# A two-layer hybrid block whose helper engines are held to a planner's order to the end of both layers

## The chip, the cores and the metric

The kernel runs on one core of a Trainium2 chip. The metric is device time in microseconds (us) from the start to the end of one execution; lower is better. The kernel before takes 1624.94 us, the median of three runs from 1623.77 to 1626.47. Five engines are named below: TensorE (PE, matmuls), VectorE (DVE), ScalarE (ACT), GpSimd (POOL) and SyncE (SP, which issues the transfers).

## What is computed

The reference runs two layers over 512 latent tokens and 256 context tokens of width 1024. Each layer mixes tokens (layer 0 with windowed attention, layer 1 with differential attention) and then runs a squared-ReLU MLP. Modulation vectors for shift, scale and gate come from a conditioning vector.

```python
def sqrelu_mlp(h, w1, w2):
    return jnp.square(jax.nn.relu(h @ w1)) @ w2

for i in range(DEPTH):
    mod_x = jax.nn.silu(c) @ w_ada[i] + b_ada[i]
    sh1, sc1, g1, sh2, sc2, g2 = jnp.split(mod_x[:, None, :], N_MOD, axis=-1)
    hx = x * (1.0 + sc1) + sh1
    ax, ac = window_gqa(...) if i % 2 == 0 else diff_attention(...)
    x = layer_norm(alpha * x + g1 * ax, ln1_g[i], ln1_b[i])
    fx = sqrelu_mlp(x * (1.0 + sc2) + sh2, mlp_w1[i], mlp_w2[i])
    x = layer_norm(alpha * x + g2 * fx, ln2_g[i], ln2_b[i])
    # layer 0: the same for the context tokens, with their own modulation
```

All data are float32. The MLP is 1024 to 4096 to 1024.

## The kernel before, in words

Every float32 product is made of three matmuls. A weight tile is brought in as `w_raw`, ACT casts it to the rounded format `w_h` (line 318), DVE subtracts to get the remainder `w_l` (line 324), and `mm3` (lines 335 to 337) multiplies w_h by the rounded activations, w_l by the same, and w_h by the remainder of the activations. So each weight needs one ACT and one DVE instruction before PE can use it.

Both MLPs work on 6 blocks of 128 tokens in layer 0 (4 of latents and 2 of context) and 4 in layer 1. Their first products partly use a scheme with fewer multiplications (Strassen-like): sums of weight tiles (`w_sum`, made by POOL at line 278) and sums of activations (`hx_sum`) are multiplied instead of the tiles, and the results (`h_ps`) are put together by adds (`relu<-h_ps`). The weights of that part are half tiles of 512 columns, `w_half`, cast at line 771 and split at line 773. The second product (`y_ps`) adds into `fx`, block by block. `y_weights(c, half)` asks for the weights of the second product of part c.

At the end of a layer's MLP, `last_y` does this: for the halves that are already complete, `fold` lets POOL compute fx times the gate row and add it to `acc` (alpha * x); `final` then takes the last piece of the second product from PSUM, multiplies it by the gate row (`g_tmp`, line 594) and adds it to acc; then come the statistics (`bn`, `mv`, `rstd`; the power of `rstd` is taken by POOL), the normalisation (line 545) and, in layer 0, the transposes `xn_t` (line 560) which feed the next layer's projections (`qkv_ps`). The gate row is made from the modulation `mods` by a transpose on PE (`gate_t`, line 467), a store to `gate_d` and a load as a row on all partitions (`g`). The modulation of the layer's second part and of layer 1 is itself computed on DVE beside the MLP of layer 0, by custom instructions on `w_raw` with the conditioning vector (`CUSTOM_DVE` at line 684, shown as ISA in orders of instructions).

The order of the work is made by a planner when the program is built. A class `Flow` runs through the jobs with estimated durations, for PE's time T and for queues A (ACT), D (DVE), G (POOL) and Q (SP). A `Ring` counts the free buffers of a tag in this plan. Where `fl.pin` names an engine and an instruction was given with `ins`, the plan's order becomes a hard order on that engine; with `fl.loose` the weight conversions are given without `ins`, so they are placed by program order and data alone. In the kernel before, `loose` is set in layer 0 after the first products of the MLP, and in layer 1 `pin` is emptied there.

Of the kernel before, what the change touches and what calls it, by code (L numbers as in the profile page):

```python
# [13 lines left out]
F32 = mybir.dt.float32  # L14
# [5 lines left out]
P = 128  # L20
# [47 lines left out]
class Flow:  # L68
# [177 lines left out]
def hybrid_block(ctx: ExitStack, tc: tile.TileContext, t: dict, out: bass.AP):  # L246
# [63 lines left out]
    def wsplit(src, n=1024, raw=None, hl=None, pool=False):  # L310
        if raw is None:
            raw = raw_tile()
        if hl is None:
            hl = [wpool.tile([P, 1024], F32R, name="w_" + x, tag="w" + x, bufs=NH) for x in "hl"] + [rwh.get(), rwh]
        raw, rg, rr = raw
        h, l, hg, hr = hl
        q = dma(n, [rg], out=raw[:, :n], in_=src)
        last["cast"] = nc.scalar.copy(out=h[:, :n], in_=raw[:, :n])  # L318
        a = fl.op("A", act(n), [q, hg], ins=None if fl.loose else last["cast"])
        kw = dict(out=l[:, :n], in0=raw[:, :n], in1=f(h)[:, :n], op=ALU.subtract)  # L320
        if pool:
            d = gp(pool2(n), [a], nc.gpsimd.tensor_tensor, **kw)
        else:
            last["split"] = nc.vector.tensor_tensor(**kw)  # L324
# [3 lines left out]
        rel.ring = hr  # L328
        return Weight(h, l, d, rel)

    last = {}

# [188 lines left out]
    def bcast_load(pool, src, nm, c0=0, n=BC):  # L521
        b = pool.tile([P, D], F32, name=nm, tag="bc", bufs=n)
        reload(b, src, c0)
        return b
# [195 lines left out]
    def mlp_pipe(l, hx, ready, ntok, acc, get_gates, done, fx, T, R):  # L720
# [40 lines left out]
        def part_sums(q):  # L761
            (a1, g1, f1), (a2, g2, f2) = R.pair_raws(q)
            q1 = dma(1024, [g1], out=a1, in_=t["w1"][l, 2 * q])
            q2 = dma(1024, [g2], out=a2, in_=t["w1"][l, 2 * q + 1])
            ws = R.sum_tile()
            (a11, a12), (a21, a22), (s1, s2) = [(x[:, 0:512], x[:, 512:1024]) for x in (a1, a2, ws)]

            def half(src, dep):
                nhalf[0] += 1
                w = R.half_tile(nhalf[0] - 1)  # L770
                a = nc.scalar.copy(out=w[:, 0:512], in_=src)  # L771
                a = fl.op("A", act(512), [dep, R.rhalf.get()], ins=None if fl.loose else a)
                d = nc.vector.tensor_tensor(out=w[:, 512:1024], in0=src, in1=f(w)[:, 0:512], op=ALU.subtract)  # L773
                d = fl.op("D", dve(512), [a], ins=None if fl.loose else d)
                rel = Task()
                rel.ring = R.rhalf
# [139 lines left out]

        gates, st, Wy, fresh, folds = [], {}, {}, set(), {}

# [57 lines left out]
        def last_y():  # L976
            def final(half, tb, pt, p, slot):
                r = gated_add(R.pool, lambda x: sm_.give(slot, x), acc[tb], half, pt, p, gates[0 if tb < NXB else 1],
                              half == 1 or l == 0, more=[folds[half, tb]])
                st[tb], r = stats(acc[tb], half, r, st.get(tb))  # L980
# [19 lines left out]
            yield from before(1)  # L1000
            halves = (1,) if gates else (0, 1)
            if not gates:
                gates.extend((yield from get_gates()))
            for half in halves:
                for tb in range(ntb):
# [62 lines left out]
        if l:  # L1068
            yield from plain(range(4), cuts)
            yield from plain((4, 5), [slice(0, ntok)], sums, 4)  # L1070
        else:
            yield from plain((0, 1), cuts, step=R.step)
            R.swap()
            for ft in range(2, 6):
                yield from plain((ft,), [t1, t2], sums, (3, 3, 2, 1)[ft - 2])
            for _ in sums:
                pass
        y_weights(0, 0)
        if l == 0:
            y_weights(0, 1)  # L1080
        if l == 0:
            fl.loose = True
        else:
            fl.pin = ""
        weights(3, 4)
        y_weights(0, 1)
        yield from steps(R.first)
        for q in range(3, 16):
            if q == R.gate_at:
                gates += yield from get_gates()  # L1090
            if q == 4 and l == 0:
                st2["second"] = True
# [421 lines left out]
    with tc.tile_pool(name="mlp0", bufs=1, reuse_waits="tile") as pool:  # L1514
# [33 lines left out]
        class R0:  # L1548
            rhalf = Ring(fl, 3)
            first, mixes = 2 * NTB, ((2, 2, 2, 0), (2, 5, 5, 0), (4, 4, 4, 0))  # L1550
# [9 lines left out]
            def half_tile(self, n):  # L1560
                p_, tag, b = ((pool, "bc", 2), (wpool, "wh", NH), (wpool, "wl", NH))[n % 3]
                return p_.tile([P, 1024], F32R, name="w_half", tag=tag, bufs=b)

# [98 lines left out]
    with tc.tile_pool(name="attn1", bufs=1, reuse_waits="tile") as pool:  # L1662
        EB1, XB1, SB = 5, 3, 1
        fl.loose = False
        fl.pin = "DAG"
# [342 lines left out]
    with tc.tile_pool(name="mlp1", bufs=1, reuse_waits="tile") as pool:  # L2008
# [37 lines left out]
        class R1:  # L2046
            rhalf, rbc = Ring(fl, 4), Ring(fl, 1)
            first, mixes = 4, ((2, 1, 2, 1), (2, 2, 2, 2), (2, 2, 2, 2))
# [17 lines left out]
            def half_tile(self, n):  # L2066
                p_, tag, b = (pool, "half", 3) if n % 4 else (late, "wl", 1)
                return p_.tile([P, 1024], F32R, name="w_half", tag=tag, bufs=b)

# [98 lines left out]
```

## Time and profile before

| what | value |
|---|---|
| median of three runs | 1624.94 us (1623.77 to 1626.47) |
| the profiled execution | 1628.53 us, span 1626.7 us |
| PE busy | 1570.4 us (97%) |
| DVE busy | 1144.1 us (70%), 2202 instructions |
| ACT busy | 790.2 us (49%) |
| POOL busy | 443.5 us (27%), 364 instructions |
| mean granted clock of PE | 0.992 |

In the trace, layer 0's MLP runs from about 385 to 885 us, with its reduced products until 825; layer 1's MLP runs from about 1263 to the end. The profile gives, per engine, busy time, idle time and the instruction that ended an idle time ("<-"). A window is a stretch of the span; its columns are the busy times of PE, of PE's weight loads, of DVE, ACT and POOL, then the granted clock (1.00 is full speed), the share of the DMA engines in use, and GB/s. In a timeline a row gives the start, the duration, the engine, the line and operation, output and inputs, and in brackets the idle time before it with what ended it.

### The profile page before, as it was taken

Reading aid. Unit: us, or ns where it says so; the run is one execution under the profiler, and the core shown is the slowest. Engines: PE = TensorE matmul, PEld = TensorE weight load, DVE = VectorE, ACT = ScalarE, POOL = GpSimd, SP = SyncE. Lnnn points to the kernel's source line nnn. Section 1 sums busy time; section 2 is a strip of 40 time slices with the busy share of each in tenths; the row PEclk is TensorE's granted clock in tenths of the full one; section 3 lists DMA queues with packets and bytes.
Section 4 is the critical chain, followed back from the end, with each engine's and each line's share of the span. In section 5 each row is a group of like instructions: output and inputs, shape, how many; then the busy total and the mean of one; then the engine's idle time right before and its main releaser. Section 6 shows DMA issues by size and latency. Waiting matters only on the chain.

```text
span 1626.7 us, 25214 instructions
## 1 busy us (share of the span) xinstructions
PE 1570.4 (97%) x9465; PEld 1376.0 (85%) x9465; DVE 1144.1 (70%) x2202; ACT 790.2 (49%) x1679; POOL 443.5 (27%) x364
## 2 busy tenths in 40 slices
PE   7999999999999999999998999999999999999998
PEld 5887777689888888888987999999987889889896
DVE  4665676689686678967567777777765796655667
ACT  3465675465334333433525655556552655554450
POOL 1344453203211221112162123220101163222363
PEclk9999999999999999999999999999999999999999
DMA  9111551352345434444243222211132333333321
GB/s 376 47 53 34 182 169 52 120 181 99 127 141 170 143 118 148 161 131 143 91 162 118 64 72 72 72 49 40 40 110 98 117 104 104 104 104 104 104 69 61
DMA packets 66435, 181.18 MB, mean 111 GB/s; under 512 B 7368, under 2 KB 13320, under 8 KB 66312
## 3 DMA queue, kind: packets, MB, share of 16 engines
q1 hardware_dynamic: 66312, 179.56, 32.9%
q8 instruction: 74, 1.21, 0.3%
q14 instruction: 49, 0.40, 0.1%
HBM read 168.49 MB, written 11.04 MB: 110 GB/s over the span
## 4 chain that ended last, share of the span: by engine, by line
PE 48%; DVE 6%; POOL 4%; ACT 2%; issue 2%; DMA 1%; SPq 0%; DVEq 0%; POOLq 0%; ACTq 0%
PE y_ps L335 6%; PE y_ps L336 6%; PE y_ps L337 6%; PE h_ps L335 5%; PE h_ps L336 5%; PE h_ps L337 5%; PE qkv_ps L335 3%; PE qkv_ps L336 3%; PE qkv_ps L337 3%; PE s_ps L1819 2%; PE o_ps L1857 2%; POOL acc L278 1%; PE pT_ps L1885 1%; POOL w_raw L278 1%; DVE acc L272 1%
## 5 line engine op out<-in xcount | busy, mean ns | idle before, releaser
L335 PE MATMUL y_ps<-w_h,hid 128*128 128x512 f32 (+1 forms) x648 | 257.5, 397 | 2.8 <-ACT w_h L318 1.8
L336 PE MATMUL y_ps<-w_l,hid 128*128 128x512 f32 (+1 forms) x648 | 256.8, 396 | 1.8 <-DVE w_l L324 1.8
L337 PE MATMUL y_ps<-w_h,hid 128*128 128x512 f32 (+1 forms) x648 | 256.4, 396 | 0.0
L324 DVE TENSOR_TENSOR w_l<-w_raw,w_h 128x1024 fp32r<-128x1024 f32 (+1 forms) x133 | 159.9, 1212 | 55.8 <-ACT w_h L318 53.8
L318 ACT CAST w_h<-w_raw 128x1024 fp32r<-128x1024 f32 (+1 forms) x133 | 130.9, 1000 | 111.2 <-PE y_ps L337 94.4
L337 PEld LDWEIGHTS y_ps<-w_h,hid 128*128 128x128 f32 x648 | 123.3, 190 | 29.1
L335 PEld LDWEIGHTS y_ps<-w_h,hid 128*128 128x128 f32 x648 | 123.5, 191 | 28.7 <-ACT w_h L318 2.6
L336 PEld LDWEIGHTS y_ps<-w_l,hid 128*128 128x128 f32 x648 | 123.3, 190 | 27.6 <-DVE w_l L324 2.9
L773 DVE TENSOR_TENSOR w_half<-w_raw,w_half 128x512 fp32r<-128x512 f32 x130 | 104.1, 808 | 59.3 <-ACT w_half L771 58.9
L771 ACT CAST w_half<-w_raw 128x512 fp32r<-128x512 f32 x130 | 79.6, 620 | 129.1 <-PE h_ps L337 91.7
L278 POOL TENSOR_TENSOR w_sum<-w_raw 128x512 f32<-128x512 f32 x26 | 45.2, 1739 | 315.6 <-DMA w_raw<-in_w 228.7
L335 PE MATMUL qkv_ps<-w_h,hx 128*128 128x384 f32 (+1 forms) x384 | 127.8, 333 | 0.3 <-ACT w_h L318 0.3
L278 POOL TENSOR_TENSOR e<-e,sm 128x512 f32<-128x512 f32 (+2 forms) x96 | 93.5, 990 | 113.8 <-DVE sm L272 81.6
L336 PE MATMUL qkv_ps<-w_l,hx 128*128 128x384 f32 (+1 forms) x384 | 122.6, 319 | 1.1 <-DVE w_l L324 1.1
L337 PE MATMUL qkv_ps<-w_h,hx 128*128 128x384 f32 (+1 forms) x384 | 122.1, 318 | 0.0
L278 POOL TENSOR_TENSOR w_raw<-w_raw,w_sum 128x512 f32<-128x512 f32 x26 | 52.4, 2016 | 187.2 <-DVE w_half L773 169.6
L684 DVE CUSTOM_DVE_ANT_0 w_raw<-w_raw,cB 128x512 f32<-128x512 f32 x112 | 90.0, 831 | 15.6 <-PE y_ps L337 13.9
L272 DVE TENSOR_TENSOR fx<-y_ps,fx 128x512 f32<-128x512 f32 x110 | 75.1, 685 | 27.1 <-PE y_ps L337 26.9
L275 ACT ACTIVATE relu<-relu 128x768 f32<-128x768 f32 (+3 forms) x104 | 69.6, 671 | 49.8 <-DVE relu L272 48.9
L278 POOL TENSOR_TENSOR rope<-rope,rope 128x256 f32<-128x256 f32 (+1 forms) x40 | 35.4, 884 | 204.8 <-DVE rope L272 140.9
L275 ACT ACTIVATE e<-e,nm 128x513 f32<-128x513 f32 (+2 forms) x96 | 65.9, 687 | 31.2 <-DVE nm L272 27.1
L335 PEld LDWEIGHTS qkv_ps<-w_h,hx 128*128 128x128 f32 x384 | 72.2, 188 | 2.6 <-ACT sk L275 1.3
(265 smaller groups left out, 4298.4 us busy)
## 6 DMA issues: line engine op xcount, KB each, us to landing
w_raw<-in_w SPq DMA_DIRECT2D x128, 512.0 KB, 3.6
w_raw<-in_w_adaT SPq DMA_DIRECT2D x56, 512.0 KB, 3.8
w_raw<-in_w_ada SPq DMA_DIRECT2D x24, 512.0 KB, 4.0
w_raw<-in_b_w SPq DMA_DIRECT2D x32, 384.0 KB, 4.1
raw<-in_w_ada SPq DMA_DIRECT2D x16, 512.0 KB, 9.5
w_raw<-in_a_wq SPq DMA_DIRECT2D x8, 512.0 KB, 8.5
w_raw<-in_a_wo SPq DMA_DIRECT2D x8, 512.0 KB, 5.5
w_raw<-in_b_wo SPq DMA_DIRECT2D x8, 512.0 KB, 4.2
```

What stands on the lines that cost most here:

```text
L272: return fl.op("D", dve(n), deps, lat, fn(**kw))
L275: return fl.op("A", act(n), deps, lat, fn(**kw))
L278: return fl.op("G", us, deps, lat, fn(**kw))
L318: last["cast"] = nc.scalar.copy(out=h[:, :n], in_=raw[:, :n])
L324: last["split"] = nc.vector.tensor_tensor(**kw)
L335: nc.tensor.matmul(out=o, lhsT=lh, rhs=rh, start=start, stop=False, **kw)
L336: nc.tensor.matmul(out=o, lhsT=lh, rhs=rl, start=False, stop=False, **kw)
L337: last["pe"] = nc.tensor.matmul(out=o, lhsT=ll, rhs=rh, start=False, stop=stop, **kw)
L684: i = fn(**kw)
L771: a = nc.scalar.copy(out=w[:, 0:512], in_=src)
L773: d = nc.vector.tensor_tensor(out=w[:, 512:1024], in0=src, in1=f(w)[:, 0:512], op=ALU.subtract)
L1819: nc.tensor.matmul(out=sp[:, c * 512:c * 512 + 384], lhsT=qTt[:, tt, hl, qb * P:(qb + 1) * P], rhs=kS[:, tt, c * 384:c * 384 + 384], start ...
```

## The change

There are five edits.

1. The plan counts buffers that two kinds of tiles share. In layer 0 two of three half tiles of weights live in the buffers of w_h and w_l. There are now two rings, `rwh` and `rwl`, and these half tiles draw on them; each conversion that takes such a buffer also follows, in the plan, the one before it (`first`, `firsth`), while the flag `mix` is set.
2. With that, `loose` is no longer set in layer 0's MLP, and `pin` is no longer emptied in layer 1's: ACT, DVE and POOL are held to the plan's order to the end of both layers.
3. The plan lets the folds wait for the load of the gate row (`gate_in`).
4. In layer 0 the second-half folds on POOL go (12 instructions). Instead, DVE adds fx to the PSUM piece, multiplies by the gate row and adds to acc: three instructions in place of two, for six blocks.
5. The weights of the first second product, `y_weights(0, 0)`, are asked for one round of first products sooner.

```diff
@@ conversions of weights
-            hl = [... for x in "hl"] + [rwh.get(), rwh]
+            hl = [... for x in "hl"] + [(rwh.get(), rwl.get()), (rwh, rwl)]
+        hg, lg = hg or (None, None)
+        turn = first if lg and fl.mix else [None]
+        turnh = firsth if lg and fl.mix else [None]
...
-        a = fl.op("A", act(n), [q, hg], ins=None if fl.loose else last["cast"])
+        a = fl.op("A", act(n), [q, hg, *turnh], ins=None if fl.loose else last["cast"])
+        turnh[0] = a
...
-            d = fl.op("D", dve(n), [a], ins=None if fl.loose else last["split"])
+            d = fl.op("D", dve(n), [a, lg, *turn], ins=None if fl.loose else last["split"])
+        turn[0] = d
@@ half tiles
-                w = R.half_tile(nhalf[0] - 1)
+                w, ring = R.half_tile(nhalf[0] - 1)
...
-                a = fl.op("A", act(512), [dep, R.rhalf.get()], ins=None if fl.loose else a)
+                a = fl.op("A", act(512), [dep, ring.get()] + (first if ring is rwl else firsth if ring is rwh else []), ins=None if fl.loose else a)
@@ fold
-            d = gp(pool2(512), [d], nc.gpsimd.tensor_tensor, out=x, in0=x, in1=g[:, cs_], op=ALU.mult)
+            d = gp(pool2(512), [d, *gate_in], nc.gpsimd.tensor_tensor, out=x, in0=x, in1=g[:, cs_], op=ALU.mult)
@@ last_y, final
+                if l == 0 and half:
+                    cs_, g = slice(512, 1024), gates[0 if tb < NXB else 1]
+                    tm = R.pool.tile([P, 512], F32, name="g_tmp", tag="tmp", bufs=tmpb[0])
+                    m = dv(512, [p], nc.vector.tensor_tensor, out=tm, in0=pt, in1=fx[tb][:, cs_], op=ALU.add)
+                    sm_.give(slot, m)
+                    m = dv(512, [m], nc.vector.tensor_tensor, out=tm, in0=tm, in1=g[:, cs_], op=ALU.mult)
+                    r = dv(512, [m], nc.vector.tensor_tensor, out=acc[tb][:, cs_], in0=acc[tb][:, cs_], in1=tm, op=ALU.add)
...
-            halves = (1,) if gates else (0, 1)
+            halves = (1,) if l else (0,)
@@ the MLP
         if l:
             yield from plain(range(4), cuts)
+            y_weights(0, 0)
             yield from plain((4, 5), [slice(0, ntok)], sums, 4)
...
             for ft in range(2, 6):
+                if ft == 5:
+                    y_weights(0, 0)
...
-        if l == 0:
-            fl.loose = True
-        else:
-            fl.pin = ""
+        fl.mix = l == 0
@@ rings
-            rhalf = Ring(fl, 3)
+            rhalf = Ring(fl, 1)
...
-            rhalf, rbc = Ring(fl, 4), Ring(fl, 1)
+            rhalf, rwl1, rbc = Ring(fl, 3), Ring(fl, 1), Ring(fl, 1)
```

PE runs the same matmuls; four groups of them change places. DVE runs 2210 instead of 2204 instructions, POOL 357 instead of 369, by the programs' own count. Line numbers are higher by some 11 to 30 in the changed kernel.

On POOL at the end of layer 0, where fx is multiplied by the gate row (g20 and g21) and added to acc0, before: the last six of 24 folds stand ahead of the first rstd.

```order
L278 TENSOR_TENSOR acc0_7897<-acc0_7897,fx_3760 128x512
L278 TENSOR_TENSOR acc0_7898<-acc0_7898,fx_3761 128x512
L278 TENSOR_TENSOR fx_3762<-fx_3762,g21_7995 128x512
L278 TENSOR_TENSOR fx_3763<-fx_3763,g21_7995 128x512
L278 TENSOR_TENSOR acc0_7899<-acc0_7899,fx_3762 128x512
L278 TENSOR_TENSOR acc0_7900<-acc0_7900,fx_3763 128x512
L278 TENSOR_TENSOR rstd_8178<-rstd_8178,mhalf_74 128x1
```

And in the changed kernel the same place, from the tenth of 12 folds on:

```order
L289 TENSOR_TENSOR fx_3763<-fx_3763,g21_7995 128x512
L289 TENSOR_TENSOR acc0_7899<-acc0_7899,fx_3762 128x512
L289 TENSOR_TENSOR acc0_7900<-acc0_7900,fx_3763 128x512
L289 TENSOR_TENSOR rstd_8167<-rstd_8167,mhalf_74 128x1
L289 TENSOR_TENSOR rstd_8190<-rstd_8190,mhalf_74 128x1
L289 TENSOR_TENSOR rstd_8213<-rstd_8213,mhalf_74 128x1
```

The twelve folds of the second half are gone; rstd follows the first twelve directly.

On PE near the end of layer 0's reduced products, before: the last gate transpose (`gate_t_7731`) stands behind a later group of y matmuls.

```order
L335 MATMUL y_ps_7717<-w_h_7582,hid_4087 128x512
L336 MATMUL y_ps_7717<-w_l_7583,hid_4087 128x512
L337 MATMUL y_ps_7717<-w_h_7582,hid_4087 128x512
L467 MATMUL gate_t_7731<-identr_73,mods1_82 8x128
L335 MATMUL h_ps_7655<-hx0m_3757,w_half_7592 128x384
```

In the changed kernel the same transpose (now `gate_t_7680`) stands 30 rows sooner, right behind the group that ends in y_ps_7628; DVE's custom instructions for this gate wait for the last matmul ahead of it.

```order
L351 MATMUL y_ps_7628<-w_h_7582,hid_4087 128x512
L352 MATMUL y_ps_7628<-w_l_7583,hid_4087 128x512
L353 MATMUL y_ps_7628<-w_h_7582,hid_4087 128x512
L483 MATMUL gate_t_7680<-identr_73,mods1_82 8x128
L351 MATMUL y_ps_7635<-w_h_7582,hid_4087 128x512
```

The gate transpose before it goes the other way, 30 rows later.

On DVE in the last 15 us of the program, before: `rstd` of the third block (acc1_12800) stands ahead of its first scale, and the fourth block's g_tmp between the two scales.

```order
L272 BN_AGGR mv_16257<-bn_16226 128x2
L272 TENSOR_SCALAR rstd_16259<-mv_16257 128x1
L272 SCALAR_TENSOR_TENSOR acc1_12800<-acc1_12800,mv_16257,l2g_16156 128x1024
L594 TENSOR_TENSOR g_tmp_16278<-y_ps_16265,g2x_14895 128x512
L272 SCALAR_TENSOR_TENSOR acc1_12800<-acc1_12800,rstd_16259,l2b_16158 128x1024
L272 BN_STATS bn_16281<-acc1_12801 128x6
L272 TENSOR_TENSOR g_tmp_16310<-y_ps_16285,g2x_14895 128x256
```

In the changed kernel (the third block is acc1_12794 there):

```order
L610 TENSOR_TENSOR g_tmp_16272<-y_ps_16259,g2x_14889 128x512
L283 BN_AGGR mv_16251<-bn_16220 128x2
L283 SCALAR_TENSOR_TENSOR acc1_12794<-acc1_12794,mv_16251,l2g_16150 128x1024
L283 TENSOR_SCALAR rstd_16253<-mv_16251 128x1
L283 BN_STATS bn_16275<-acc1_12795 128x6
L283 SCALAR_TENSOR_TENSOR acc1_12794<-acc1_12794,rstd_16253,l2b_16152 128x1024
L283 COPY bn3_16277<-bn_16275 128x6
L283 TENSOR_TENSOR g_tmp_16304<-y_ps_16279,g2x_14889 128x256
```

The g_tmp went ahead of the aggregate, rstd behind the first scale, and the fourth block's statistics between the two scales; POOL's power of rstd now also stands behind the fourth block's add there.

More of the change, by code (lines that the diff above doesn't have):

```diff
@@ L80, in __init__ @@
         self.prev, self.order, self.pin, self.loose, self.low = {}, None, "", False, False
+        self.mix = False
     def pe(self, us):
@@ L193, in back, with __init__ @@
             self.free.append(at)
+class Both:
+    def __init__(self, *rings):
+        self.rings = rings
+    def back(self, at):
+        for r in self.rings:
+            if r is not None:
+                r.back(at)
 YES, NO = 0.0, 1e18
@@ L522, in bcast_load @@
         b = pool.tile([P, D], F32, name=nm, tag="bc", bufs=n)
-        reload(b, src, c0)
+        queue["row"] = reload(b, src, c0)
         return b
@@ L769, in half @@
                 nhalf[0] += 1
-                w = R.half_tile(nhalf[0] - 1)
+                w, ring = R.half_tile(nhalf[0] - 1)
                 a = nc.scalar.copy(out=w[:, 0:512], in_=src)
-                a = fl.op("A", act(512), [dep, R.rhalf.get()], ins=None if fl.loose else a)
+                a = fl.op("A", act(512), [dep, ring.get()] + (first if ring is rwl else firsth if ring is rwh else []), ins=None if fl.loose else a)
+                if ring is rwl:
+                    first[0] = a
+                if ring is rwh:
+                    firsth[0] = a
                 d = nc.vector.tensor_tensor(out=w[:, 512:1024], in0=src, in1=f(w)[:, 0:512], op=ALU.subtract)
@@ L915, in pair @@
             yield from mix(3)
-        gates, st, Wy, fresh, folds = [], {}, {}, set(), {}
+        gates, st, Wy, fresh, folds, gate_in = [], {}, {}, set(), {}, []
         def y_weights(c, half, n=2):
@@ L977, in final @@
             def final(half, tb, pt, p, slot):
-                r = gated_add(R.pool, lambda x: sm_.give(slot, x), acc[tb], half, pt, p, gates[0 if tb < NXB else 1],
-                              half == 1 or l == 0, more=[folds[half, tb]])
+                if l == 0 and half:
[5 more added lines that the diff above has]
+                    r = dv(512, [m], nc.vector.tensor_tensor, out=acc[tb][:, cs_], in0=acc[tb][:, cs_], in1=tm, op=ALU.add)
+                else:
+                    r = gated_add(R.pool, lambda x: sm_.give(slot, x), acc[tb], half, pt, p, gates[0 if tb < NXB else 1],
+                                  half == 1 or l == 0, more=[folds[half, tb]])
                 st[tb], r = stats(acc[tb], half, r, st.get(tb))
@@ L1000, in last_y @@
             yield from before(1)
-            halves = (1,) if gates else (0, 1)
+            halves = (1,) if l else (0,)
             if not gates:
                 gates.extend((yield from get_gates()))
+                gate_in.append(queue["row"])
             for half in halves:
@@ L1090, in mlp_pipe @@
                 gates += yield from get_gates()
+                gate_in.append(queue["row"])
             if q == 4 and l == 0:
@@ L1560, in half_tile @@
             def half_tile(self, n):
-                p_, tag, b = ((pool, "bc", 2), (wpool, "wh", NH), (wpool, "wl", NH))[n % 3]
-                return p_.tile([P, 1024], F32R, name="w_half", tag=tag, bufs=b)
+                p_, tag, b, ring = ((pool, "bc", 2, self.rhalf), (wpool, "wh", NH, rwh), (wpool, "wl", NH, rwl))[n % 3]
+                return p_.tile([P, 1024], F32R, name="w_half", tag=tag, bufs=b), ring
             def relu_tile(self):
@@ L1663, in hybrid_block @@
         EB1, XB1, SB = 5, 3, 1
-        fl.loose = False
+        fl.loose = fl.mix = False
         fl.pin = "DAG"
@@ L2066, in half_tile @@
             def half_tile(self, n):
-                p_, tag, b = (pool, "half", 3) if n % 4 else (late, "wl", 1)
-                return p_.tile([P, 1024], F32R, name="w_half", tag=tag, bufs=b)
+                p_, tag, b, ring = (pool, "half", 3, self.rhalf) if n % 4 else (late, "wl", 1, self.rwl1)
+                return p_.tile([P, 1024], F32R, name="w_half", tag=tag, bufs=b), ring
             def relu_tile(self):
```

12 lines of the change are left out of this document (6 added, 6 removed).

## The prediction

> **What bounds the kernel now.** I read the page's busy times first, then TensorE's (PE's) waits, then the windows with their granted clock, then the timelines around the places that the change moves.
>
> ```profile
> span 1626.7 us, 25214 instructions
> PE 1570.4 (97%) x9465; PEld 1376.0 (85%) x9465; DVE 1144.1 (70%) x2202; ACT 790.2 (49%) x1679; POOL 443.5 (27%) x364
> ```
>
> PE is the bound: 1626.7 − 1570.4 leaves 56.3 us, and the matmuls are the same before and after; SP issues the same transfers with a few swapped by one or two places, so raw rows land as now. So the change can win only waits of PE, the half-speed stretches that follow long waits, and the tail behind the last matmul. PE's waits, in total us, count and longest, and the windows (clock after the five engines):
>
> ```profile
> PE xn_t L560 <- DVE acc L545: 4.2, 1, 4.2
> PE y_ps L336 <- DVE w_l L324: 2.5, 5, 0.8
> PE gate_t L467 <- DVE mods L272: 2.0, 1, 2.0
> PE y_ps L335 <- ACT w_h L318: 1.8, 2, 1.2
> PE y_ps L335 <- DVE fx L272: 1.0, 1, 1.0
> ...
> 700.00:750.00 50.00, 47.96 (x234) 42.81 (x233) 33.57 (x67) 18.15 (x29) 6.32 (x4) 0.97 0.42 137
> 850.00:900.00 50.00, 45.47 (x224) 38.73 (x223) 36.26 (x67) 27.30 (x76) 16.20 (x14) 0.93 0.35 119
> 1300.00:1350.00 50.00, 46.96 (x261) 41.02 (x260) 44.83 (x52) 27.27 (x48) 27.17 (x9) 0.93 0.33 111
> 1345.00:1626.70 281.70, 273.83 (x1675) 243.95 (x1673) 179.22 (x250) 126.90 (x223) 101.74 (x65) 1.00 0.28 94
> ```
>
> The rows name places that the change touches: the normalisation at the end of layer 0 (xn_t), the gate's transpose, and the conversions of MLP weights. A single wait of 2 us already costs clock: 700:750 stands at 0.97, so 0.03 × 50 = 1.5 us are lost beside the wait itself. From 1345 on the clock is whole and PE waits for nothing until its last matmul.
>
> **Part 1, the end of layer 0.** The longest wait, with POOL, VectorE (DVE) and PE from the timeline and two rows from the chain of waits:
>
> ```profile
> 825.96 2.54 POOL L278 TENSOR_TENSOR fx<-fx,g 128x512 f32<-128x512 f32 x2 [30.81 <-DMA g<-gate_d]
> 843.75 3.00 POOL L278 TENSOR_TENSOR fx<-fx,g 128x512 f32<-128x512 f32 x2
> 862.91 0.54 POOL L278 TENSOR_TENSOR rstd<-rstd,mhalf 128x1 f32<-128x1 f32 x1
> 858.67 0.15 DVE L272 TENSOR_SCALAR rstd<-mv 128x1 f32<-128x1 f32 x1
> 863.49 0.81 DVE L545 TENSOR_SCALAR acc<-acc,mv,rstd 128x1024 f32<-128x1024 f32 x1 [2.88 <-POOL rstd L278]
> 884.28 0.96 DVE L324 TENSOR_TENSOR w_l<-w_raw,w_h 128x768 fp32r<-128x768 f32 x1 [0.24 <-ACT w_h L318]
> ...
> 864.36 1.97 PE L560 MATMUL xn_t<-identr,acc 128*128 128x128 f32 x8 [4.23 <-DVE acc L545]
> ...
> 866.33 0.43 PE y_ps L335
> 870.24 0.24 PE y_ps L336
> 870.71 0.87 PE xn_t L560 x8
> ```
>
> DVE has its variance at 858.8, but POOL takes up rstd only at 862.91, when 24 folds that began at 825.96 (as the gate's row landed) are through. PE stands for 4.23 us and then runs slow: the first eight transposes take 1.97 us where the next eight take 0.87 (1.1 lost), and matmuls step at 0.43 instead of 0.24 from 866.33 until some eight are done (8 × 0.19 = 1.5). The stop costs 4.23 + 2.6 = 6.8 us.
>
> The change takes 12 of the 24 folds away. In the present trace the twelfth ends at 843.75, 19 us before rstd is wanted. DVE instead gets one instruction more for each of six blocks; the two that lie ahead of the first normalisation cost 2 × 0.68 = 1.4. So rstd can go at about 858.8 + 1.4 and normalisation ends near 860.2 + 0.5 + 0.8 = 861.5. PE reaches its xn_t later: before at 864.36 − 4.23 = 860.1, now behind 12 more y matmuls of 0.234, 862.9. The stop should go whole: −6.8.
>
> Not all of it stays. In the new order the fifth block's normalisation and the splits of layer 1's first qkv weights stand on DVE behind the last blocks' multiply and add (a split takes 0.96, a two-input instruction on 512 columns 0.68, as in the rows at 1320.67 below), and only 1 to 3 us of matmuls lie between what those adds wait for and the matmuls that need the splits. Walking DVE's queue with these rows I get new waits of 0.9 (block five), 1.2 (three splits) and 1.6 (the fifth pair, whose raw buffer comes free only with a split): +3.6. Bounds 0, if contention gone from DVE (below) pays for it, and 5.5, if they also slow the clock by a 700:750's worth. Net −3.2, from −6.8 to −1.3.
>
> **Part 2, conversions in layer 0's MLP.** PE's rows that the moved conversions end, and two each of ACT's and DVE's:
>
> ```profile
> 401.78 0.50 PE L335 MATMUL y_ps<-w_h,hid 128*128 128x512 f32 x1 [0.62 <-ACT w_h L318]
> 403.04 0.50 PE L336 MATMUL y_ps<-w_l,hid 128*128 128x512 f32 x1 [0.76 <-DVE w_l L324]
> 491.55 0.49 PE L335 MATMUL y_ps<-w_h,hid 128*128 128x512 f32 x1 [1.18 <-ACT w_h L318]
> 642.93 0.44 PE L335 MATMUL h_ps<-hx0m,w_half 128*128 128x384 f32 x1 [0.63 <-DVE relu L272]
> 654.87 0.44 PE L335 MATMUL h_ps<-hx_sum,w_half 128*128 128x384 f32 x1 [0.43 <-ACT relu L275]
> 704.85 0.28 PE L467 MATMUL gate_t<-identr,mods 128*8 128x128 f32 x1 [2.04 <-DVE mods L272]
> 798.32 0.44 PE L335 MATMUL h_ps<-hx0m,w_half 128*128 128x384 f32 x1 [0.79 <-DVE relu L272]
> ...
> 487.81 1.72 ACT L275 ACTIVATE relu<-relu 128x768 f32<-128x768 f32 x2 [4.49 <-DVE relu L272]
> 490.45 1.04 ACT L318 CAST w_h<-w_raw 128x1024 fp32r<-128x1024 f32 x1 [0.92 <-DMA w_raw<-in_w]
> ...
> 793.92 1.78 DVE L684 CUSTOM_DVE_ANT_0 w_raw<-w_raw,cB 128x512 f32<-128x512 f32 x1
> 795.63 0.68 DVE L684 CUSTOM_DVE_ANT_0 w_raw<-w_raw,cB 128x512 f32<-128x512 f32 x1
> ```
>
> The first y weights are asked for one round sooner; their casts and splits move ahead of a dozen matmuls' worth of other work: −0.62 − 0.76 = −1.4. At 599.8 an fx add moves ahead of two weight splits (the 1.0 in the waits): −1.0. At 642.93 a relu add moves ahead of one: −0.6. Against this, ScalarE (ACT) now holds its order. At 491.55 the cast of w_h, which now starts as its raw rows land, stands behind one more square of 768 columns (0.86) and two shorter steps: with the gap of 0.92 filled, 1.2 later, up to 2.7 if the longer stop also slows the clock. At 654.87 the copy of relu stands behind a square and a hid cast more, while another hid cast moves ahead of it: about one such operation net, +1.0, from 0 to 2.5.
>
> The gates change places. The transpose at 704.85 goes 30 PE rows later and its wait disappears: −2.04 − 1.5 of clock = −3.5. The one for (1, 5), which waits next to nothing now, goes 30 rows earlier, right behind the last y matmul that frees its raw rows, so the two DVE reductions and the two adds behind them lie bare. Their nearest price is the same work at 793.92: 1.78 + 0.08 + 0.68 + 0.08 and 0.4 for the adds, 3.0, with 1.5 of clock: +4.5 (bounds 3.5, as at 704.85, and 5.6, if POOL slows both reductions). The 0.79 at 798.32 is then over: −0.8. Sum of part 2: −1.4 − 1.0 − 0.6 + 1.2 + 1.0 − 3.5 + 4.5 − 0.8 = −0.6, from −4.5 to +4.
>
> **Part 3, layer 1.** The waits at the start of its MLP, behind the group of all such adds:
>
> ```profile
> L278 POOL TENSOR_TENSOR w_raw<-w_raw,w_sum 128x512 f32<-128x512 f32 x26 | 52.4, 2016 | 187.2 <-DVE w_half L773 169.6
> ...
> 1307.54 14.94 POOL L278 TENSOR_TENSOR w_raw<-w_raw,w_sum 128x512 f32<-128x512 f32 x1 [6.79 <-ACT hx1m L275]
> 1320.67 0.68 DVE L773 TENSOR_TENSOR w_half<-w_raw,w_half 128x512 fp32r<-128x512 f32 x1
> 1324.46 0.58 PE L335 MATMUL h_ps<-hx_sum,w_half 128*128 128x256 f32 x1 [3.04 <-ACT relu L275]
> ```
>
> A POOL add that takes some 1.5 elsewhere ((52.4 − 14.9) / 25 from the group's row) takes 14.94 here, and it ends 1.1 us after the last of a row of DVE instructions without a gap (1320.67 + 0.68). ACT's cast waits for it, the copy of relu stands behind the cast, and PE waits for the copy. The change moves the token sums ahead of the w_half splits, so POOL's add may start later, near 1312, but the same instructions still follow on DVE without a wait up to the same split. I leave this wait at 0 change; if one gap opens it goes, which is worth between 3.04 and 3.04 + 0.07 × 50 of clock = 6.5; I take the middle, 4.7.
>
> [...]
>
> In the middle of layer 1 orders move, but PE has no wait to lose there, and between each copy's input and its use stand 12 y matmuls at 0.24, 2.8 us, mostly with 12 narrower ones; the copies moved by one conversion each keep within that. In the tail DVE's last pieces are:
>
> ```profile
> 1613.38 1.52 POOL L278 TENSOR_TENSOR rstd<-rstd,mhalf 128x1 f32<-128x1 f32 x1 [3.94 <-DVE rstd L272]
> 1615.23 2.20 POOL L278 TENSOR_TENSOR acc<-acc,g_tmp 128x512 f32<-128x512 f32 x1 [0.34 <-DVE g_tmp L594]
> 1617.47 0.69 DVE L272 BATCH_NORM_STATS2 bn<-acc 128x6 f32<-128x512 f32 x1 [1.19 <-POOL acc L278]
> 1618.08 0.41 DVE L272 TENSOR_TENSOR g_tmp<-y_ps,g2x 128x256 f32<-128x256 f32 x1
> ```
>
> Now rstd of block three comes behind the 1.2 us scale on DVE and behind POOL's 2.2 us add, and the last scale waits for it ahead of the closing g_tmp. Walked with these rows, that g_tmp starts near 1618.9 instead of 1618.08: +0.8 (0 to 1.5).
>
> **Sum.** −3.2 − 0.6 + 0 + 0.8 = −3.0 us on the profiled execution (1628.53, of which 1626.7 span). It lies 3.6 above the median of the runs shown, 1624.94, and outside their range, so I take the same 3.0 off the median: 1621.9. The unknowns lean to a gain (each new wait was charged in full), so I say **1621.5**.
>
> **Rivals.** *A, a larger gain:* part 1's new waits are hidden, since 12 folds fewer on POOL also shorten DVE (1.78 against 0.68 above), and one gap lets POOL's add through: −3.0 − 3.6 − 4.7 = −11.3, 1613.6; either alone gives 1617 to 1618. For it: DVE is idle 14 of 50 us in 850:900. Against: 44.83 of 50 in 1300:1350. [...] *B, no change:* the stop at 864 goes but DVE, with six instructions more, is late at blocks four to six by what was won: part 1 at 0, so +0.2, 1625.1. For it: the splits' short leads. *C, slower:* with ACT and DVE held to the plan's order in both MLPs, a conversion that waits for POOL or its DMA holds up the relu copies behind it, as 1324.46 shows; the plan does not know that DVE stretches POOL. Each such place costs 4.7; it decides once a POOL add ends later than the 2.8 us of cover. Two of them: −3.0 + 9.4 = +6.4, 1631.3. For it: POOL and DVE collide at 793.92. Against: only one such place shows now, and the order there stays.
>
> **Numbers.** Forecast 0.45 (own range 1619 to 1624), A 0.20, B 0.13, C 0.22. About 0.2%, 3.2 us, is what a measurement can tell from no change. The forecast lies at that border: 0.27 of it beyond, 0.18 within. Faster 0.27 + 0.20 = 0.47, same 0.18 + 0.13 = 0.31, slower 0.22. The range 1613 to 1629.5 takes in A's sum and C with one place and a half.
>
> **What would show it.** Right: no xn_t wait above 1 us near 860, POOL idle between its folds and rstd, the waits at 402 gone, a new gate_t wait of 2 to 4 us near 790, the POOL add near 1312 still long, the last g_tmp nearly a us later behind PE's end. Wrong: a w_half or relu wait of over 2 us in 440:800 that is new, or qkv waits that sum to more than 4 us at 885 to 900.

## The result, and the profile after

The change takes 1638.42 us (median of four runs, 1637.11 to 1639.93) against 1624.97 before (four runs, 1623.77 to 1626.47): ratio 1.008, 95% interval 1.0065 to 1.0094. It is 13.4 us slower, outside the predicted range and on the other side of no change. The profiled execution took 1639.69 us with a span of 1637.9, 11.2 longer than the span before: the profiled execution of before lies 3.6 above its median, that of the change 1.3 above its own.

Two of TensorE's (PE's) waits before, which the prediction's list leaves out:

```profile
PE h_ps L335 <- ACT relu L275: 5.7, 4, 3.0
PE h_ps L335 <- DVE relu L272: 2.9, 3, 1.5
```

After, the page's lines on the span and the busy times, and PE's waits that answer to these and to those shown of before:

```profile
span 1637.9 us, 25184 instructions
PE 1571.3 (96%) x9465; PEld 1373.9 (84%) x9465; DVE 1137.8 (69%) x2208; ACT 786.3 (48%) x1679; POOL 414.8 (25%) x352
...
PE h_ps L351 <- ACT relu L286: 10.4, 9, 2.7
PE h_ps L351 <- DVE relu L283: 3.9, 3, 2.1
PE gate_t L483 <- DVE mods L283: 3.8, 1, 3.8
PE qkv_ps L352 <- DVE w_l L339: 2.5, 6, 0.9
...
PE xn_t L576 <- DVE acc L561: 1.0, 2, 0.8
```

PE's busy time is the same within 1 us, and POOL has the 12 folds fewer. The 4.2 us wait at the normalisation is gone, but the products `h_ps` wait longer and more often for relu, on ScalarE (ACT) 10.4 us instead of 5.7 and on VectorE (DVE) 3.9 instead of 2.9. To see where the time went I matched the same matmuls in both traces and took how much later each one starts in the change. The points are taken where the same number of transposes has run in both traces; only at 796 the change has already run one that the kernel before runs next:

| matmul at (us, before) | starts later by | step, and what lies in it |
|---|---|---|
| 400 | -0.8 | |
| 442 | -2.7 | -1.9: the waits at 401 and 403 gone |
| 537 | +1.2 | +3.9: waits near 445, 460 and 526 longer or new, with slow matmuls behind the first |
| 651 | -0.1 | -1.3: the wait at 599.8 gone |
| 666 | +6.2 | +6.3: wait for ACT's relu 2.72 instead of 0.43, slow matmuls, and 1.2 for a new wait of 0.91 for fx behind them |
| 701 | +6.9 | +0.7: new wait of 0.42 for w_l |
| 719 | +3.1 | -3.8: the gate's transpose at 704.85 no longer waits |
| 742 | +3.9 | +0.8: new wait of 0.53 |
| 796 | +10.2 | +6.3: a new wait of 0.43 near 785 (0.7), then gate (1, 5), which waits 3.83, and slow matmuls (5.6) |
| 807 | +8.9 | -1.3: the wait at 798.32 gone, with the transpose that stood ahead of it |
| 883 | +1.3 | -7.6: the stop at 864 gone (6.9 of it) |
| 906 | +5.1 | +3.8: new waits for block five and for the qkv splits |
| 1346 | +5.8 | +0.7: start of layer 1's MLP |
| last matmul | +6.7 | +0.9: new wait near 1601 |
| end | +11.2 | +4.4: the tail behind the last matmul |

The traces differ by up to 3 us before layer 0's MLP begins (this offset, taken at 330, lies between 0 and -3 in all the kernels below), so steps are read here, not levels. A step is larger than the wait in it: the waits at 401 and 403 are 0.62 and 0.76 us, and with them 1.9 us go, so each costs some 0.25 us more than its idle time.

**Near 654.** ACT's timeline of the kernel before, then ACT and PE of the changed kernel:

```profile
648.77 0.85 ACT L275 ACTIVATE relu<-relu 128x768 f32<-128x768 f32 x1 [6.78 <-DVE relu L272]
...
652.08 0.83 ACT L275 CAST hid<-relu 128x768 fp32r<-128x768 f32 x1
652.82 0.52 ACT L275 ACTIVATE relu<-relu 128x384 f32<-128x384 f32 x1
653.24 1.12 ACT L771 CAST w_half<-w_raw 128x512 fp32r<-128x512 f32 x2
654.34 0.48 ACT L275 COPY relu<-h_ps 128x384 f32<-128x384 f32 x1
654.72 0.85 ACT L275 ACTIVATE relu<-relu 128x768 f32<-128x768 f32 x1
```

```profile
649.44 1.73 ACT L286 ACTIVATE relu<-relu 128x768 f32<-128x768 f32 x2 [7.47 <-DVE relu L283]
...
654.56 0.84 ACT L286 ACTIVATE relu<-relu 128x768 f32<-128x768 f32 x1
655.31 0.60 ACT L787 CAST w_half<-w_raw 128x512 fp32r<-128x512 f32 x1
655.82 0.83 ACT L286 CAST hid<-relu 128x768 fp32r<-128x768 f32 x1
656.55 0.47 ACT L286 COPY relu<-h_ps 128x384 f32<-128x384 f32 x1
...
657.07 0.69 PE L351 MATMUL h_ps<-hx_sum,w_half 128*128 128x384 f32 x1 [2.72 <-ACT relu L286]
657.56 0.52 PE L352 MATMUL h_ps<-hx_sum,w_half 128*128 128x384 f32 x1
657.88 0.52 PE L353 MATMUL h_ps<-hx_sum,w_half 128*128 128x384 f32 x1
```

The copy that PE waits for stood ahead of the last square of 768 columns and behind one hid cast; now that square and two hid casts stand ahead of it, two operations more (some 1.5 us), and the chain that leads there begins 0.67 later (649.44 against 648.77). After the wait, matmuls step at 0.32 us until about 663.

**Gate (1, 5).** DVE and PE of the changed kernel:

```profile
795.50 1.65 DVE L700 CUSTOM_DVE_ANT_0 w_raw<-w_raw,cB 128x512 f32<-128x512 f32 x1 [4.75 <-PE y_ps L353]
...
797.08 1.74 DVE L700 CUSTOM_DVE_ANT_0 w_raw<-w_raw,cB 128x512 f32<-128x512 f32 x1
...
799.06 0.17 DVE L283 TENSOR_TENSOR mods<-mods,c_badaT 128x8 f32<-128x8 f32 x1
...
799.29 0.28 PE L483 MATMUL gate_t<-identr,mods 128*8 128x128 f32 x1 [3.83 <-DVE mods L283]
```

**The tail.** POOL, DVE and PE of the changed kernel:

```profile
1596.64 3.98 POOL L289 TENSOR_TENSOR fx<-fx,g2x 128x512 f32<-128x512 f32 x2
...
1607.07 2.53 POOL L289 TENSOR_TENSOR acc<-acc,fx 128x512 f32<-128x512 f32 x2
1609.57 1.29 POOL L289 TENSOR_TENSOR acc<-acc,g_tmp 128x512 f32<-128x512 f32 x1
...
1610.89 0.69 DVE L610 TENSOR_TENSOR g_tmp<-y_ps,g2x 128x512 f32<-128x512 f32 x1 [5.45 <-POOL acc L289]
...
1629.24 0.42 DVE L283 TENSOR_TENSOR g_tmp<-y_ps,g2x 128x256 f32<-128x256 f32 x1
...
1625.28 0.28 PE L353 MATMUL y_ps<-w_h,hid 128*128 128x256 f32 x1
```

POOL still folds until 1609.6; DVE stands for 5.45 us and its closing g_tmp comes 4.0 behind the start of the last matmul. Before it began 0.5 ahead of it (1618.08 against 1618.55).

### The profile page after: what moved, and what is told of

It reads as the page before. It is cut to its first block, busy times and chain, and to the rows that moved or that the text cites. A ratio compares the mean times of both kernels' runs of the same rounds, so it can differ in the third digit from the quotient of the medians.

```text
span 1637.9 us, 25184 instructions
## 1 busy us (share of the span) xinstructions
PE 1571.3 (96%) x9465; PEld 1373.9 (84%) x9465; DVE 1137.8 (69%) x2208; ACT 786.3 (48%) x1679; POOL 414.8 (25%) x352
## 4 chain that ended last, share of the span: by engine, by line
PE 75%; DVE 11%; ACT 6%; issue 4%; POOL 3%; DMA 2%; SPq 0%; DVEq 0%; ACTq 0%; POOLq 0%
PE y_ps L352 9%; PE y_ps L353 9%; PE y_ps L351 9%; PE h_ps L351 6%; PE h_ps L352 6%; PE h_ps L353 6%; PE qkv_ps L351 3%; PE qkv_ps L352 3%; PE qkv_ps L353 3%; PE o_ps L1451 2%; PE s_ps L1849 2%; PE pT_ps L1469 2%; PE o_ps L1887 2%; ACT relu L286 1%; DVE w_l L339 1%
## 5 line engine op out<-in xcount | busy, mean ns | idle before, releaser
L289 POOL TENSOR_TENSOR w_raw<-w_raw,w_sum 128x512 f32<-128x512 f32 x26 | 45.6, 1754 | 224.8 <-DVE w_half L793 185.5
L286 ACT COPY relu<-h_ps 128x384 f32<-128x384 f32 (+1 forms) x78 | 33.0, 423 | 91.2 <-PE h_ps L353 91.2
```

Of the source, the lines that this page charges most:

```text
L286: return fl.op("A", act(n), deps, lat, fn(**kw))
L289: return fl.op("G", us, deps, lat, fn(**kw))
```

## The experiments

Times are medians; each group of experiments had its own runs of the kernel before, with medians from 1625.3 to 1626.7 us. Against them the ratio is given, with its 95% interval.

**The tail.** Theory: POOL, tied in layer 1, takes the folds too late. Rival: DVE's order.

*All of layer 1's MLP free again:*

```diff
         fl.mix = l == 0
+        if l:
+            fl.pin = ""
```

> The change, but in layer 1's MLP the plan's order binds no engine (pin emptied there, as before). Theory (POOL's folds of the second half, held behind those of the first half, make DVE wait 5.45 us and lose the tail): PE's offset of +1.6 us gathered in 1300 to 1605 and the +4.5 us behind the last matmul both go, 1638.4 - 5.5 = 1632.9, with no DVE wait on POOL above 1.5 us after 1600. Rival (the loss in layer 1 is only handed on from layer 0, as a shifted phase): under 1 us gained, 1637.5 to 1638.5.

Measured: 1631.95, ratio 1.003 (1.0018 to 1.0042). The tail behind the last matmul is back to 7.9 us from 12.3.

*POOL alone free:* the orders of ACT, DVE, PE and SP are those of the change.

```diff
         fl.mix = l == 0
+        if l:
+            fl.pin = "DA"
```

> The change, with only POOL free of the plan's order in layer 1's MLP; ACT and DVE stand exactly as in the change. Theory (POOL's order of folds is the cause of the lost tail): the folds go back between 1565 and 1595, the 5.45 us wait goes, 4 to 5 us are won, 1633.5 to 1634.5. Rival (DVE's new order in the tail, rstd behind the scale and g_tmp ahead, is the cause): DVE's order is unchanged, so at most 1 us, 1637.5 to 1638.5.

Measured: 1630.72, ratio 1.0027 (1.0018 to 1.0037); span 1629.9. POOL, DVE and PE of this run:

```profile
1546.72 1.30 POOL L289 TENSOR_TENSOR fx<-fx,g2x 128x512 f32<-128x512 f32 x1
...
1591.62 2.15 POOL L289 TENSOR_TENSOR acc<-acc,fx 128x512 f32<-128x512 f32 x1
1597.37 1.29 POOL L289 TENSOR_TENSOR acc<-acc,g_tmp 128x512 f32<-128x512 f32 x1 [3.59 <-DVE g_tmp L610]
...
1621.25 0.42 DVE L283 TENSOR_TENSOR g_tmp<-y_ps,g2x 128x256 f32<-128x256 f32 x1
...
1621.42 0.28 PE L353 MATMUL y_ps<-w_h,hid 128*128 128x256 f32 x1
```

Three pairs of folds run between POOL's adds of weights from 1546.72 on, all eight are done by 1593.8, and the closing g_tmp is 0.2 ahead of the last matmul's start again. In the tied order all eight pairs stand behind the last add of weights, at 1574.58 or later. With DVE's order unchanged the tail is 8.2: POOL's order is the cause, shown. The new wait near 1601 goes with it. Both runs won more than their theory said, 6.5 and 7.7 us by the medians against 5.5 and 4 to 5. Near 654, which neither edit touches, their traces lose 4.2 and 2.3 us where the change's loses 6.3, so part of it may be chance (the last section takes this up).

**Layer 0 from 440 to 805.** Theory at first: the tied conversions hold up what stands behind them.

*The ties of layer 0's conversions taken off, the rest of the change kept (PE's order is that of the change):*

```diff
         fl.mix = l == 0
+        if l == 0:
+            fl.loose = True
```

> The change, but in layer 0's MLP weight conversions are again given without a place in the plan's order; PE's order is that of the change, the moved gate included. Theory (holding the conversions to the plan is what costs in 440:800: relu copies at 654 behind a square and a cast, the waits at 445, 526, 670): the new waits there go, about 8 us, but the gate's 3.8 us wait at 795 stays: 1630 to 1631. Rival (the loss there is the plan's new order on PE and the modulation work on DVE): 0 to 3 us, 1635.5 to 1638.5.

Measured: 1636.13, ratio 1.0052 (1.0037 to 1.0067). The losses at 445 to 537 are gone (offset -4.9 at 442, -4.4 at 537), but other waits come. Two of PE's rows and its gate row:

```profile
596.71 0.80 PE L351 MATMUL y_ps<-w_h,hid 128*128 128x512 f32 x1 [2.30 <-DVE fx L283]
...
654.37 0.49 PE L351 MATMUL h_ps<-hx_sum,w_half 128*128 128x384 f32 x1 [1.93 <-ACT relu L286]
...
794.96 0.38 PE L483 MATMUL gate_t<-identr,mods 128*8 128x128 f32 x1 [5.87 <-DVE mods L283]
```

From 442 to 807 this kernel still loses 9.3 us where the change loses 11.6. The median falls into the rival's range: the theory holds for 445 to 537, and at 654, where the wait is 1.93 and not 2.72, for the smaller part of the wait; the rest does not hang on the ties. I formed another: the order that the plan gives once it counts the shared buffers.

*The counting alone:* the kernel before with edit 1 of the change; loose and pin as before, no folds on DVE, no weights sooner.

```diff
-    rwh = Ring(fl, NH)
+    rwh, rwl = Ring(fl, NH), Ring(fl, NH)
...
+        fl.mix = l == 0
         if l == 0:
             fl.loose = True
         else:
             fl.pin = ""
```

> The kernel before with the new counting of shared buffers in the plan alone: nothing is tied, no fold on VectorE, no weights sooner. On TensorE only the two gates change places; on ScalarE the copies of relu in 640:700 stand behind a square and a hid cast. Theory (the new plan's order costs by itself): about as much as the change loses in 640:800, a relu wait near 654 of 2 us or more with slow matmuls behind it (+2.5 to +6), the gate at 704.85 won (-3.5) and the one near 795 lost (+5.5), in sum +4.5 to +8, 1629.5 to 1633. Rival (the losses come from tying the conversions, the plan itself is harmless): within 1.5 us of the kernel before, 1623.5 to 1626.5.

Measured: 1634.34, ratio 1.005 (1.0034 to 1.0066). PE:

```profile
655.90 0.44 PE L351 MATMUL h_ps<-hx_sum,w_half 128*128 128x384 f32 x1 [1.95 <-ACT relu L286]
...
793.89 0.38 PE L483 MATMUL gate_t<-identr,mods 128*8 128x128 f32 x1 [5.47 <-DVE mods L283]
```

By the medians the plan alone costs about 8 us, a little more than the theory's 8 at most, and both places show it with nothing tied: +1.5 near 654, where the wait is 1.95 and no slow matmuls follow, and +6.3 at the gate near 795, against -3.8 at the gate near 705. The profiled run was this kernel's fastest of six (1631.23), so its trace shows less than the median: +6.4 from 442 to 807. Of these 1.7 lie at 491, where slow matmuls follow a wait of 1.33 (1.18 before).

*The change with gate (1, 5) asked for later in the plan; on PE only that row moves:*

```diff
     def ada_gate(l, m, dep):
+        if (l, m) == (1, 5):
+            yield dep
+            yield fl.T + 6.0
```

> The change, with the request for the transpose of gate (1, 5) put off by 6 us in the plan; on TensorE only that one row moves. Theory (the transpose lies bare, right behind the matmul that frees the raw rows of its reductions): its wait of 3.8 us and the slow matmuls behind it go, 5 us in all (4 to 6), so 1633.5 us against 1638.4 of the change. Rival (the wait is handed on: VectorE's reductions hold up what the next matmuls need, as at 798.32 of the kernel before): at most 1.5 us are won, 1637 or more.

Measured: 1633.15, ratio 1.0043 (1.0031 to 1.0055), as the theory said. The row reads, without a wait:

```profile
796.59 0.27 PE L483 MATMUL gate_t<-identr,mods 128*8 128x128 f32 x1
```

From 742 to 807 it loses nothing, where the change loses 5.0. The profiled run was the fastest of nine, which go from 1629.57 to 1637.76.

*Both mends together:*

```diff
+        if (l, m) == (1, 5):
+            yield dep
+            yield fl.T + 6.0
...
+        if l:
+            fl.pin = "DA"
```

> The change with both mends: the transpose of gate (1, 5) put off by 6 us in the plan, and POOL not held to the plan's order in layer 1's MLP. Theory (the losses are separate places, each of which came out by itself): 1638.4 - 5.3 - 7.7 = 1625.4 us, within 2 us, so no difference from the kernel before. Rival (the two share a loss, or one uncovers another): 1629 or more.

Measured: 1628.42, ratio 1.0014 (1.0005 to 1.0023). Between theory and rival: 3 us short of the sum. The wait at 654 is 2.72 here too and cost 6.4 with its slow matmuls and a wait for fx behind them; in the traces of the two single mends it cost 2.3. How often it takes which course I did not settle, and so not whether that is the whole 3 us.

*And the copy near 654 ahead of that square:*

```diff
-            d = ac(c.stop - c.start, d, nc.scalar.activation, out=r[:, c], in_=r[:, c], func=AF.Relu)
+            d = ac(c.stop - c.start, d, nc.scalar.activation, lat=1.2 if (l, q, fi) == (0, 9, 1) else LAT, out=r[:, c], in_=r[:, c], func=AF.Relu)
```

> As the run with both mends, and in the plan the last square of one pair of hidden blocks (the one near 654 us) starts 1 us later, so that ScalarE's copy of relu stands ahead of a w_half cast, that square and a hid cast instead of behind them; six rows of ScalarE and a few of VectorE change places, none of TensorE. Theory (what the plan put ahead of the copy is the wait of 2.7 us near 654): that wait falls below 0.7 us and the slow matmuls behind it go: 2 to 6 us less than the run with both mends. Rival (the copy waits for something that is late by itself, such as VectorE's relu add): less than 1 us won.

Measured: 1626.3, ratio 1.0006 (0.9996 to 1.0015), 2.1 less than with two mends. ACT and PE:

```profile
654.38 0.61 ACT L790 CAST w_half<-w_raw 128x512 fp32r<-128x512 f32 x1
654.89 0.48 ACT L286 COPY relu<-h_ps 128x384 f32<-128x384 f32 x1
655.26 0.63 ACT L790 CAST w_half<-w_raw 128x512 fp32r<-128x512 f32 x1
655.78 0.86 ACT L286 ACTIVATE relu<-relu 128x768 f32<-128x768 f32 x1
...
655.42 0.44 PE L351 MATMUL h_ps<-hx_sum,w_half 128*128 128x384 f32 x1 [0.74 <-ACT relu L286]
```

The wait is 0.74, just above the 0.7 that the theory allowed, and the slow stretch is gone: what the plan put ahead of the copy was the wait. With three places mended, 12 of the 13.4 us are back, and the change stands level with the kernel before.

**The parts that were to gain, each alone on the kernel before.**

*The folds on DVE:*

```diff
+                if l == 0 and half:
+                    cs_, g = slice(512, 1024), gates[0 if tb < NXB else 1]
+                    tm = R.pool.tile([P, 512], F32, name="g_tmp", tag="tmp", bufs=tmpb[0])
+                    m = dv(512, [p], nc.vector.tensor_tensor, out=tm, in0=pt, in1=fx[tb][:, cs_], op=ALU.add)
...
-            halves = (1,) if gates else (0, 1)
+            halves = (1,) if l else (0,)
```

> The kernel before with the last folds of layer 0 on VectorE and nothing else of the change. Theory (part 1 of the prediction): the stop at 864 goes, -6.8, and waits at 870 to 890 take 2 to 5.5 of it back, so 1 to 5 us faster than before, 1620 to 1624. Rival (VectorE's six additional instructions hand the whole wait to blocks four to six): 1625 or more.

Measured: 1626.73, ratio 1.0005 (0.9992 to 1.0017): nothing. The stop at 864 is gone (-7.5 from 807 to 883), and 8.4 come back by 906, most of it at this row and in the slow matmuls behind it:

```profile
886.38 1.94 PE L560 MATMUL xn_t<-identr,acc 128*128 128x128 f32 x8 [5.43 <-DVE acc L545]
```

The rival had it, with a detail it lacked: the plan now puts block six's transposes behind 6 qkv matmuls, where the kernel before has 42 and the change 24. PE meets block six before DVE has it ready; that the plan takes DVE for quicker than it is, I read from this order, and its own times are not shown.

*The weights sooner:*

```diff
             for ft in range(2, 6):
+                if ft == 5:
+                    y_weights(0, 0)
```

> The kernel before with the first second-network weights of layer 0 asked for one round sooner, alone; six rows of ScalarE and of VectorE change places, none of TensorE. Theory (part 2's first step): the waits near 402 go, -1.4, 1622.5 to 1625 beside 1626. Rival (the waits are handed to the relu of the next block): no difference in the trace behind 460 us.

Measured: 1622.9, ratio 0.9978 (0.9968 to 0.9988). The waits at 401 and 403 are gone and nothing comes back by 651. The trace shows 1.9 at that place. Another 1.5 lie at the gate near 704.85: PE waits the same 2.04 there, but in this execution no slow matmuls follow. No edit touches that place, so what the sooner weights are shown to bring is 1.9; the rest of the 3.2 has no row that belongs to them.

*Both together:* the two diffs above on the kernel before.

> The kernel before with two edits only: the second-half folds of layer 0 on DVE, and y_weights(0, 0) asked for a round sooner in layer 0. No plan with shared buffers, no new ties. Theory (these two are gains by themselves, as measured in the change between PE's rows: -1.9 us at 402 and -3.8 us from 855 to 905): 1625.0 - 5.7 = 1619.3. Rival (these gains come from the plan's new order around them; alone, DVE's six instructions more give back what POOL saves): 1623 to 1626.

Measured: 1624.9, ratio 0.9985 (0.9975 to 0.9994): faster by 2.4 by that ratio, within the rival's range, and no more than the sooner weights alone.

**A version that beats both.** The last kernel with two rows of PE put later in the plan: gate (1, 2), as the change has it, and block six's transposes, behind 30 qkv matmuls.

```diff
+        if (l, m) == (1, 2):
+            yield dep
+            yield fl.T + 6.0
...
-                          LNLAT), 0)
+                          LNLAT + 5.0 * (tb == 5)), 0)
```

> The kernel before with the folds on VectorE and the first second-network weights one round sooner (the run that came out at 1624.9 beside 1626.7 of before), and with two rows of TensorE put later: the last block's transposes behind 24 qkv matmuls more, the transpose of gate (1, 2) behind 30 rows more. Theory: the wait of 5.4 us at the last block's transposes and its slow matmuls go (-4 to -6), and so does the gate's of 2 us (-2 to -3.5): 6 to 9 us under the run without the two, about 1616 to 1619. Rival (the VectorE splits that the qkv matmuls need become the wait instead): at most 3 us won, 1622 or more.

Measured: 1619.18, ratio 0.9953 (0.9938 to 0.9968), 7.6 us (0.47%) under the kernel before by that ratio, 6.8 by the medians. Against the run without the two rows put later it wins some 5 us by the ratios, short of the 6 to 9 of the theory. The gate's wait is gone (offset -3.6 at 701, -7.3 at 719). At the transposes the rival was half right: the stop becomes two waits for splits,

```profile
878.51 0.44 PE L335 MATMUL qkv_ps<-w_h,hx 128*128 128x384 f32 x1 [1.53 <-ACT w_h L318]
880.59 0.44 PE L336 MATMUL qkv_ps<-w_l,hx 128*128 128x384 f32 x1 [1.64 <-DVE w_l L324]
```

and from 807 to 906 it wins 1.8 where the run without the two wins 0.6.

*The same without the folds on DVE and with the transposes where the kernel before has them:*

```diff
+                if ft == 5:
+                    y_weights(0, 0)
...
+        if (l, m) == (1, 2):
+            yield dep
+            yield fl.T + 6.0
```

> The kernel before with the first second-network weights of layer 0 one round sooner and the transpose of gate (1, 2) behind 30 rows more of TensorE: the run that came out at 1619.2 us, without the folds on VectorE and without the later transposes of the last block. Theory (the folds on VectorE bring little: alone they came out even, since VectorE's six more instructions hand the wait on): 3.2 us of the sooner weights and 2 to 3.5 of the gate, 1619.5 to 1621, within 1.5 us of that run. Rival (with the last block's transposes later, the folds do win their part 1): 1622 or more.

Measured: 1621.14, ratio 0.9967 (0.9956 to 0.9978), at the upper end of what the theory said. The gate's row and the sooner weights give most of the gain; the folds with the later transposes are worth some 2 us by the medians, and the two intervals overlap.

The ties without the counting were not tried.

## Why the prediction was wrong, step by step

**Part 1 was right.** -3.2 was said, -3.8 measured (807 to 906): the stop gone whole (-6.9 against -6.8, with 0.7 more just ahead of it) and +3.8 of new waits against 3.6. The single waits are shorter than said: block five waits 0.78 against 0.9, three splits 0.5 against 1.2 and the fifth pair 0.90 against 1.6; what each wait costs beyond its idle time makes up for that, and it had no term, so that the 3.6 came out so close is in part luck. The walk used the change's own order of transposes, and the sum hangs on it: with the same folds and block six's transposes behind 6 qkv matmuls it is +0.8, and behind 30, with the gate moved, -1.8.

**Part 2 was wrong by some 10 us:** -0.6 said, +9.7 measured (400 to 807). Of its terms 401/403 (-1.9 against -1.4), 599.8 (-1.3 against -1.0), the gate at 704.85 (-3.8 against -3.5) and 798.32 (-1.3 against -0.8) came out near. The -3.8 is counted from the one trace of before, in which slow matmuls follow the gate's wait; in the traces of the runs with the folds alone, the weights sooner and both, the same wait has none and costs 1.5 less. Three steps failed:

- *654.87, "about one such operation net, +1.0, from 0 to 2.5".* Measured +6.3. The net count was wrong, since two operations and not one came ahead of the copy (1.5 us), and I missed that the chain into them starts 0.67 later. For the slow matmuls behind the wait, which I had charged at the gate and in the bound at 491, the +1.0 had no term; with the wait for fx behind them they took 4.0. The experiment with the copy put back shows the place as the cause.
- *The gate (1, 5), +4.5, bounds 3.5 to 5.6.* Measured +5.6 (787 to 796): right in kind, at the upper bound. The wait is 3.83 and not 3.0, because I priced the second reduction at 0.68, as in the row at 795.63, and it took 1.74.
- *445 to 537 had no term.* Measured +3.9; the run without the ties loses 0.5 there, and with the ties PE waits 2.09 near 445 where it waits 1.49 without them, so these waits come from the ties. (The run with the plan alone loses 2.1 there, 1.7 of it at 491, where it waits 1.33 against 1.18 before, with slow matmuls behind.) I had walked only the rows that wait in the kernel before, and a reordered queue makes waits where there were none. 491, charged at +1.2, came out near zero, and 642.93 kept its wait of 0.6.

**Part 3:** the start came out at +0.7 against 0, and for the reason given: POOL's add begins later and still ends 1.1 us behind the last of DVE's row.

```profile
1318.18 10.14 POOL L289 TENSOR_TENSOR w_raw<-w_raw,w_sum 128x512 f32<-128x512 f32 x1 [12.21 <-ACT hx_sum L286]
1326.51 0.68 DVE L793 TENSOR_TENSOR w_half<-w_raw,w_half 128x512 fp32r<-128x512 f32 x1
```

The tail, +0.8 (0 to 1.5), measured +5.4 with the wait near 1601. (The middle of layer 1 cost nothing, as said: +5.8 at 1346 and at 1590.) I took DVE's new order for the whole of it and left POOL's folds where they ran, though the change ties POOL as well; its order had moved eight pairs of folds behind the last add of weights, and the group's row of before had shown POOL idle for 187.2 us ahead of its 26 adds: gaps in which a free POOL can fold and a tied one cannot.

**The rivals.** C had the sign and one of the places' kind (a relu copy held up on ACT), but not its mechanism: no POOL add ends late there, the plan's own order does it, and it does it untied. Its share of 0.22 was too low, as I see it because I priced the plan's new order only at places that already waited. A and B fell.

**What would show it.** The signs named for "right" came at five of six places: xn_t's longest wait 0.78, the waits at 402 gone, a gate_t wait of 3.83, the POOL add still long, POOL free for rstd. The sixth, "nearly a us later behind PE's end", was 4.4, and the first sign for "wrong", a new relu wait above 2 us in 440:800, came (2.72; and 2.09 near 445, where 1.49 stood).

## What to carry to other kernels

A plan that is made more truthful in one respect still orders by its guesses in the others. Here it put two more ScalarE operations ahead of a copy that PE needs, and a transpose right behind the matmul that its own inputs wait for. That it believed DVE and ACT to be early is my reading of these orders; the plan's own times are not shown here. Before a queue is tied to a plan, look at what the free queue did in its idle gaps, on every engine the tie covers; POOL's folds in the gaps were worth the whole tail. When a stop is taken away by moving work to another engine, check where the consumer was moved as well: the same folds were worth nothing with one block's transposes early and 3.8 us at their place in the change.

## What the runs showed of the hardware

The same wait does not cost the same. Near 654 PE waits 2.72 in the change and 2.69 in the run with the later gate; there the rows go on:

```profile
655.42 0.44 PE L351 MATMUL h_ps<-hx_sum,w_half 128*128 128x384 f32 x1 [2.69 <-ACT relu L286]
655.70 0.34 PE L352 MATMUL h_ps<-hx_sum,w_half 128*128 128x384 f32 x1
655.88 0.34 PE L353 MATMUL h_ps<-hx_sum,w_half 128*128 128x384 f32 x1
```

The steps are 0.18 us there; in the change they are 0.32. The window 650 to 700 of the change, then of that run:

```profile
650.00:700.00 50.00, 45.95 (x211) 40.52 (x210) 38.78 (x86) 20.46 (x34) 6.88 (x5) 0.93 0.44 146
```

```profile
650.00:700.00 50.00, 46.53 (x224) 40.34 (x223) 39.25 (x87) 19.47 (x33) 9.65 (x7) 1.00 0.46 152
```

So a wait of 2.7 us cost 6.3 in one trace (with the wait for fx that followed) and 2.3 in another. Shorter waits have two prices as well. The gate's wait of 2.04 near 704 leaves a granted clock of 0.91 in 700 to 720 of the kernel before, and of 1.00 in the three runs that keep it (the folds alone, the weights sooner, both). Near 491 PE waits twice, 1.0 to 1.4 us and some 0.8 right behind: in 490 to 500 the clock is 0.83 with POOL alone free and with the folds alone, and 1.00 in the kernel before and with both mends. In the clock records of the kernel before and of the change, each slow stretch between the first 20 us and the last matmul lasts 3.41 or 6.83 us at half clock (3.41 at 705.85 and 6.83 at 862.86 before, 3.41 at 799.75 and 6.83 at 656.39 in the change), so it costs up to 1.7 or 3.4 us. For a sum it means that waits of some 1 to 2.7 us had more than one price here, and that one profile shows one of them.
